# Delta-rule stage of a hybrid encoder layer: TensorE's order pinned over two streams, and the solved blocks turned on VectorE instead of through DRAM

## The chip, the cores and the metric

One core of a Trainium2 chip. The time is device microseconds of one execution of the whole kernel; the time of a kernel is the median of its runs. The profile comes from one further execution.

## The reference

One layer over 1024 positions of width 1024, in float32. The token mixing has a gated DeltaNet branch with 8 heads of 128 and a band attention branch with 16 heads; then come the branch projections, a LayerNorm, a gated feed-forward net with a short convolution, and another LayerNorm. The change lies in the DeltaNet branch:

```python
qkv = jax.nn.silu(causal_dwconv(qkv, conv_w))          # 4 taps
q = l2norm(q) * (A_DK ** -0.5); k = l2norm(k)
beta = sigmoid(beta_raw); g = -exp(a_log) * softplus(a_raw + dt_bias)
...
a_low = where(strict, einsum("bnhid,bnhjd->bnhij", k_beta, k) * decay, 0.0)
rhs = concatenate([v_beta, k_beta * exp(g)[..., None]], axis=-1)
sol = lax.linalg.triangular_solve(a_low + eye, rhs, left_side=True, lower=True, unit_diagonal=True)
u, w = sol[..., :dv], sol[..., dv:]
def step(state, inp):
    v_new = u_n - einsum("bhck,bhkv->bhcv", w_n, state)
    o_n = (einsum("bhck,bhkv->bhcv", q_n * exp(g_n)[..., None], state)
           + einsum("bhij,bhjv->bhiv", qk_n, v_new))
    state = state * exp(g_last)[..., None, None] + einsum("bhck,bhcv->bhkv", k_dec, v_new)
    return state, o_n
```

So each head has, chunk by chunk, the inverse of a unit lower triangular matrix and a recurrence over the chunks, which is serial. The kernel takes chunks of 128 positions, eight per head.

## The kernel before

Everything is held with channels on the 128 partitions. A projection multiplies in three passes: the input h and each weight block are split into a high and a low part (hh, hl; wh, wl), and `mm_fm` issues hh x wh, hl x wh and hh x wl for each of 8 pieces of the contraction. That makes 24 matmuls of 128x512 into one bank of PSUM, and 48 for a block of 128 output columns over 1024 positions. These matmuls (`pqkv`, `pz`, `pgt`, `pqk`, line L284) are the bulk of TensorE's work; they are called projection matmuls or dense matmuls here. The weight block comes by a DMA to `raw`; ScalarE casts it to `wh` (L177), and GpSimd subtracts to get `wl` (L180).

The delta-rule stage runs head by head. For a head:

- `stage_k`: decays `mm` and `gb` (L564 to L569, with an Exp of 128x1024 on ScalarE at L567), projection and convolution of k (`conv_in`, L554 is its Silu), transposes, the matrix `am` = k k^T with beta and decay; its 32x32 diagonal blocks go out to DRAM (`fa_d`, L609) and come back as `fa` (part of the buffer G) with one block per partition (L613). GpSimd puts -1 on their diagonals (L615).
- `stage_q`, `stage_vz`: the projections of q, v and z, transposes, scores `at`, scaled values `vs` (`pv`, L654).
- `stage_solve`: the 32 blocks (4 diagonal blocks in each of 8 chunks) are inverted row by row on VectorE: 31 times a TENSOR_TENSOR (L670) and a TENSOR_REDUCE (L672), each on the result of the one before. The result `ft` (FT) goes to DRAM in four writes (`ft_d`, L674) and comes back in four reads as blocks on the diagonal of `dt_` (part of G, L677), all on SP's DMA queue.
- `stage_inverse`, in two halves g of four chunks: VectorE transposes `dt_` to `dd` (L689), and four groups of small matmuls join 32x32 inverses to 64x64 and 128x128 ones: `pxt` (L694), `py` (L706 to L708), `pzz` (L714), `pT` (L720), with copies on ScalarE and VectorE between them (L697, L709 and their like).
- `stage_chain`: eight serial steps. In a step `pks` (L732) multiplies k by the state, VectorE updates `vs` (L733), `pvn` (L736) multiplies by the inverse, ScalarE copies to `vn` (part of SA, L739), `pu` (L742) makes the update, VectorE adds it to the state (part of SA, L747), and `po` (L750, L752) makes the output. Each of the three small matmuls pks, pvn and pu needs what an engine made of the one before; that is a hand-over, 168 in all.
- `stage_out`: the norm and the gate, and a DMA to `oa_d`.

The instructions are traced in this order: for a head h its solve, its inverse, some gate blocks (`some_gates`: projections of the merge gates and of two blocks for attention; GA says how many), k and q of head h+1, two half rows of the modulation (`mod_rows`), v and z of head h+1, the chain of head h and its output. A scheduler then sets the order on each engine by its own estimate of times, with the priorities PI, PC and PT for the inverse, the chain and the output. Nothing pins an engine's order but what `issue_after` ties. Buffers are rings of the size in the table `AT`: `xt`, `zd` and `dd` have two each.

Of the kernel before, what the change touches and what calls it, by code (L numbers as in the profile page):

```python
# [20 lines left out]
NK = 8  # L21
# [9 lines left out]
PI = 2000  # L31
PT = 2000
# [4 lines left out]
GE = ()  # L37
# [3 lines left out]
G0 = 1  # L41
GA = (3, 2, 2, 2, 3, 2, 2, 99)
# [12 lines left out]
GB = (0, 0, 0, 0, 0, 0, 0, 9)  # L55
# [7 lines left out]
def _at(group, step_, n, first=0):  # L63
# [15 lines left out]
    "tmp": tuple(_T), "dT": _at("G", 0, 1), "fa": _at("G", 0, 1, 1024), "dd": _at("G", 512, 2, 2048),  # L79
    "xt": _at("G", 256, 2, 3072), "zd": _at("G", 256, 2, 3584),  # L80
# [60 lines left out]
def hybrid_layer(  # L141
# [129 lines left out]
    def dhalf(name):  # L271
        return pbank(name, "d")
# [245 lines left out]
    def halves(name, col0, ready=None):  # L518

        w = None if ready else wblock(kview(w_in2, col0, P), NK)  # L520
        for n in range(2):
            ps = ready[n] if ready else dhalf(nm(name))
            if not ready:
                mm_fm(ps, w, hhk, hlk, n)
            yield n, slice(512 * n, 512 * n + 512), ps

    def conv_in(h, m):
        ti = m * NK + h
        y = big(f"y{m}")
# [19 lines left out]
        return y  # L549
# [6 lines left out]
    def stage_k(h):  # L556

        c = {}
# [12 lines left out]
        kT = c["kT"] = conv_in(h, 1)  # L571
        if h == 0:
            dump("kT", flat(kT))
        kd = c["kd"] = big("kd")
        ss = c["ss"] = sm("ss", 2 * NT)
        for g in range(2):
            pk = mbank("pk")
            for t in range(4):
                PE.transpose(pk[:, t, :], kT[:, 4 * g + t, :], ident)
            for t in range(4):  # L580
                u = 4 * g + t
                sumsq(ss[:, u:u + 1], pk[:, t, :])
            for t in range(4):
                u = 4 * g + t
                DVE.tensor_scalar(kd[:, u, :], pk[:, t, :], mm[:, u, P - 1:P], None, ALU.mult)
        kss = sm("kss")
        DVE.tensor_scalar(kss, ss[:, 0:NT], L2_EPS, None, ALU.add)
# [3 lines left out]
        bkk = sm("bkk")  # L591
# [4 lines left out]
        am = c["am"] = big("am")  # L596
        for g in range(2):
            pk = mbank("pkk")
            for t in range(4):
                PE.matmul(pk[:, t, :], kT[:, 4 * g + t, :], kT[:, 4 * g + t, :],  # L600
                          start=True, stop=True)
            for t in range(4):
                u = 4 * g + t
                DVE.scalar_tensor_tensor(am[:, u, :], pk[:, t, :], bkk[:, u:u + 1],
                                         mm[:, u, :], ALU.mult, ALU.mult)
        fa_d = scr.tile([4, NT, 32, 32], F32, tag="fa_d", bufs=2, name=nm("fa_d"))
        c["ft_d"] = scr.tile([4, NT, 32, 32], F32, tag="ft_d", bufs=2, name=nm("ft_d"))
# [10 lines left out]
        return c  # L618

    def stage_q(h, c):  # L620

        qT = c["qT"] = conv_in(h, 0)
        if h == 0:
            dump("qT", flat(qT))
        kT, mm, gb, ss = c["kT"], c["mm"], c["gb"], c["ss"]
        at = c["at"] = big("at")
        for g in range(2):
            G = slice(4 * g, 4 * g + 4)
            pk = mbank("pkq")
            for t in range(4):  # L630
                PE.matmul(pk[:, t, :], kT[:, 4 * g + t, :], qT[:, 4 * g + t, :],
                          start=True, stop=True)
            DVE.tensor_tensor(at[:, G, :], pk, mm[:, G, :], ALU.mult)
        for g in range(2):
            pk = mbank("pq")
            for t in range(4):
                PE.transpose(pk[:, t, :], qT[:, 4 * g + t, :], ident)
            for t in range(4):
                u = NT + 4 * g + t
                sumsq(ss[:, u:u + 1], pk[:, t, :], pk[:, t, :])  # L640
        eq = c["eq"] = sm("eq")
# [3 lines left out]
    def stage_vz(h, c):

        vT = conv_in(h, 2)
        if h == 0:
            dump("vT", flat(vT))
        vs = c["vs"] = big("vs")  # L650
        for g in range(2):
            pv = mbank("pv")
            for t in range(4):
                PE.transpose(pv[:, t, :], vT[:, 4 * g + t, :], ident)  # L654
            for t in range(4):
                u = 4 * g + t
                ACT.activation(vs[:, u, :], pv[:, t, :], AF.Copy, scale=c["bk"][:, u:u + 1])

        sz = c["sz"] = big("sz")
        for n, N, ps in halves("pz", 3 * D + h * P):  # L660
            ACT.activation(flat(sz)[:, N], ps, AF.Silu)

    def stage_solve(h, c):

        fa, ft_d = c["fa"], c["ft_d"]
        ft = ring("ft", [P, 8, 32])
        POOL.tensor_copy(ft, tt0)
        for i in range(1, 32):
            pr = ring("pr", [P, 8, 32])
            DVE.tensor_tensor(pr[:, :, 0:i + 1], ft[:, :, 0:i + 1],  # L670
                              fa[:, i:i + 1, 0:i + 1].to_broadcast([P, 8, i + 1]), ALU.mult)
            DVE.tensor_reduce(ft[:, :, i:i + 1], pr[:, :, 0:i + 1], AX.X, ALU.add, negate=True)  # L672
        for q in range(4):
            SP.dma_start(ft_d[:, :, 8 * q:8 * q + 8, :].rearrange("b t c j -> (b t) (c j)"),  # L674
                         ft[32 * q:32 * q + 32].rearrange("p c j -> p (c j)"))
        for b in range(4):
            SP.dma_start(dt_[32 * b:32 * b + 32, :, 32 * b:32 * b + 32],  # L677
                         ft_d[b].rearrange("t c j -> c t j"))

    def stage_inverse(h, c):  # L680
# [5 lines left out]
        for g in range(2):  # L686
            G = slice(4 * g, 4 * g + 4)
            dd = ring("dd", [P, 4, P])
            DVE.transpose(flat(dd), flat(dt_)[:, 512 * g:512 * g + 512])  # L689
            px_ = mbank("pxt", "i")  # L690
            for t in range(4):
                u = 4 * g + t
                for i, j in ((B0, B1), (B2, B3)):
                    PE.matmul(px_[i, t, j], am[:, u, i], dt_[:, u, j], start=True, stop=True)  # L694
            xt = ring("xt", [P, 4, 64])
            ACT.activation(xt[B0, :, 0:32], px_[B0, :, B1], AF.Copy, scale=-1.0)
            DVE.tensor_scalar(xt[B2, :, 32:64], px_[B2, :, B3], -1.0, None, ALU.mult)  # L697
            for b in (B2, B3):
                POOL.tensor_copy(am[b, G, b], dt_[b, G, b])
            POOL.memset(am[B1, G, B0], 0.0)  # L700
            POOL.memset(am[B3, G, B2], 0.0)
            for b in (B0, B1):
                POOL.tensor_copy(am[b, G, b], dt_[b, G, b])
            py = mbank("py", "i")
            for t in range(4):
                PE.matmul(py[B2, t, B3], dd[:, t, B2], xt[:, t, 32:64], start=True, stop=True)  # L706
                PE.matmul(py[B0, t, B1], dd[:, t, B0], xt[:, t, 0:32], start=True, stop=True)
                PE.matmul(py[B1, t, B0], xt[:, t, 0:32], dd[:, t, B0], start=True, stop=True)  # L708
            DVE.tensor_copy(am[B2, G, B3], py[B2, :, B3])  # L709
# [12 lines left out]

    def stage_chain(h, c):
# [3 lines left out]
        c["steps"] = []  # L727
        so = sm("so")
        for t in range(NT):
            if t:  # L730
                pks = mtile(nm("pks"), "c")
                PE.matmul(pks[:, 0:P], kT[:, t, :], st_, start=True, stop=True)  # L732
                DVE.scalar_tensor_tensor(vs[:, t, :], pks[:, 0:P], c["nbe"][:, t:t + 1],  # L733
                                         vs[:, t, :], ALU.mult, ALU.add)
            pv = mtile(nm("pvn"), "c")
            c["last"] = PE.matmul(pv[:, 0:P], am[:, t, :], vs[:, t, :], start=True, stop=True)  # L736
# [813 lines left out]
```

## Time and profile before

| | us |
|---|---|
| median of 3 runs | 2217.51 |
| lowest, highest | 2213.31, 2221.87 |
| the profiled execution | 2222.63 |
| its span in the trace | 2220.5 |
| TensorE busy in the span | 2140.7 (96%) |
| VectorE, ScalarE, GpSimd busy | 1477.9, 999.6, 500.9 |

The granted TensorE clock was 0.99 on average in the profiled execution. The page gives busy time by engine; times of single instructions are of that one execution. A busy time counts overlapped matmuls once: the 11577 matmuls take some 390 to 400 ns each by themselves (section 5), but start closer together. Idle time of an engine is put down to what came last before it could go on, written "<- engine tile line".

### The profile page before, as it was taken

The numbers are of one execution on the slowest core, as the hardware profiler recorded it, in microseconds if no ns is written. First come the engines' busy times: TensorE is split into PE (matmuls) and PEld (weight loads), VectorE is DVE, ScalarE is ACT, GpSimd is POOL, SyncE is SP. The second block draws the span as 40 slices with busy tenths as digits, with TensorE's granted clock in tenths as the row PEclk, the third lists the DMA queues.
The fourth block names the chain that finished last, engine by engine and source line by source line (L and its number), as shares of the span: only waits on it lengthen the run. The fifth ranks groups of instructions, "written<-read, shape, count | busy, mean of one in ns | idle before, by whom it ended". The sixth has DMA issues, their size and how long they took to land.

```text
span 2220.5 us, 31618 instructions
## 1 busy us (share of the span) xinstructions
PE 2140.7 (96%) x11577; PEld 1793.2 (81%) x11577; DVE 1477.9 (67%) x3096; ACT 999.6 (45%) x2127; POOL 500.9 (23%) x495
## 2 busy tenths in 40 slices
PE   7989999999999999999999899999999999999998
PEld 6778788777878787798989788888788888888886
DVE  6478476674758754567776653456998788875754
ACT  5634243443524334566765642234654444453331
POOL 0223233222323322233432422400120000000000
PEclk9999999999999999999999999999999999999999
DMA  9242323323243403211211424332232222275540
GB/s 289 86 121 71 113 80 106 110 74 110 78 120 87 128 24 99 68 51 50 72 55 60 148 96 128 114 128 95 76 102 70 78 83 86 90 260 210 171 152 38
DMA packets 227453, 232.01 MB, mean 104 GB/s; under 512 B 28058, under 2 KB 179027, under 8 KB 227299
## 3 DMA queue, kind: packets, MB, share of 16 engines
q1 hardware_dynamic: 227219, 229.98, 33.0%
q8 instruction: 91, 1.49, 0.3%
q14 instruction: 63, 0.52, 0.1%
q10 hardware_dynamic: 80, 0.03, 0.0%
HBM read 189.02 MB, written 47.23 MB: 106 GB/s over the span
## 4 chain that ended last, share of the span: by engine, by line
PE 49%; DVE 3%; ACT 1%; issue 1%; DMA 0%; POOL 0%; DVEq 0%; SPq 0%; ACTq 0%; POOLq 0%
PE pup L1268 17%; PE pdn L1422 11%; PE pbr L1049 8%; PE pwo L1110 4%; PE pqk L891 2%; PE pv L906 2%; PE po L981 2%; PE pp L966 1%; PE ps L940 1%; PE pn L1133 0%; DMA raw<-in_w_branch_a_dram 0%; DVE G L1329 0%; DVE t L170 0%; DVE kl L1011 0%; DVE pl L970 0%
## 5 line engine op out<-in xcount | busy, mean ns | idle before, releaser
L180 POOL TENSOR_TENSOR wl<-raw,wh 128x1024 fp32r<-128x1024 f32 x85 | 204.8, 2412 | 334.2 <-ACT wh L177 306.3
L1268 PE MATMUL pup<-hh,wop 128*128 128x512 f32 x704 | 224.2, 390 | 0.4 <-ACT G L1305 0.4
L1268 PE MATMUL pup<-t,wop 128*128 128x512 f32 x792 | 189.5, 392 | 1.4 <-DVE cc L1309 0.8
L1268 PEld LDWEIGHTS pup<-t,wop 128*128 128x128 f32 x792 | 148.6, 188 | 34.8 <-DVE cc L1309 1.2
L1422 PE MATMUL pdn<-dop,dop 128*128 128x512 f32 x696 | 161.6, 391 | 0.0
L177 ACT CAST wh<-raw 128x1024 fp32r<-128x1024 f32 x88 | 92.4, 1050 | 147.4 <-DMA raw<-in_w_in_dram 63.8
L1268 PEld LDWEIGHTS pup<-hh,wop 128*128 128x128 f32 x704 | 132.1, 188 | 29.1 <-ACT G L1305 0.8
L1422 PEld LDWEIGHTS pdn<-dop,dop 128*128 128x128 f32 x696 | 130.7, 188 | 28.3
L284 PE MATMUL pqkv<-hh,wh 128*128 128x512 f32 x352 | 142.8, 406 | 0.0
L284 PE MATMUL pqkv<-hl,wh 128*128 128x512 f32 x352 | 140.5, 399 | 0.0
L284 PE MATMUL pqkv<-hh,wl 128*128 128x512 f32 x352 | 140.2, 399 | 0.0
L1268 PE MATMUL pup<-hl,wop 128*128 128x512 f32 x352 | 137.2, 390 | 0.0
L670 DVE TENSOR_TENSOR FT<-FT,G 128x16 f32<-128x16 f32 (+30 forms) x248 | 121.6, 490 | 20.5 <-POOL G L615 13.1
L1310 POOL TENSOR_TENSOR cc<-cc,G 128x512 f32<-128x512 f32 x22 | 44.4, 2019 | 375.5 <-DVE G L1292 352.3
L951 POOL TENSOR_SCALAR G<-G,FT 128x640 f32<-128x640 f32 (+4 forms) x103 | 70.3, 685 | 182.4 <-DVE FT L950 161.6
L177 ACT CAST wop<-wr 128x512 fp32r<-128x512 f32 x104 | 61.9, 620 | 99.4 <-DVE wr L1250 66.9
L284 PE MATMUL pgt<-hh,wh 128*128 128x512 f32 x240 | 95.6, 399 | 0.4 <-DVE tmp L537 0.4
L284 PE MATMUL pgt<-hh,wl 128*128 128x512 f32 x240 | 94.7, 395 | 0.0
L284 PE MATMUL pgt<-hl,wh 128*128 128x512 f32 x240 | 94.7, 395 | 0.0
L180 DVE TENSOR_TENSOR wop<-wr,wop 128x512 fp32r<-128x512 f32 x104 | 75.3, 731 | 16.8 <-ACT wop L177 16.2
L970 DVE TENSOR_TENSOR pl<-pp,ph 128x512 fp32r<-128x512 f32 (+2 forms) x116 | 72.5, 635 | 17.4 <-ACT ph L969 16.6
L948 ACT ACTIVATE G<-G,FT 128x640 f32<-128x640 f32 (+4 forms) x103 | 71.6, 695 | 18.9 <-DVE FT L943 16.9
(413 smaller groups left out, 5786.2 us busy)
## 6 DMA issues: line engine op xcount, KB each, us to landing
raw<-in_w_in_dram SPq DMA_DIRECT2D x72, 512.0 KB
wr<-in_w_up_dram SPq DMA_DIRECT2D x44, 512.0 KB
dwr<-in_w_down_dram SPq DMA_DIRECT2D x44, 512.0 KB
raw<-in_w_ada_dram SPq DMA_DIRECT2D x32, 512.0 KB
wa<-in_w_ada_dram SPq DMA_DIRECT2D x32, 256.0 KB
gates_d<-GT SPq DMA_DIRECT2D x32, 256.0 KB
g_d<-G SPq DMA_DIRECT2D x15, 512.0 KB
rel_d<-in_rel_bias_dram SPq DMA_DIRECT2D x16, 383.5 KB
```

The lines of the kernel that those rows point to most:

```text
L177: he.copy(h, src)
L180: return le.tensor_tensor(l, src, f(h), ALU.subtract).ins
L284: i = PE.matmul(ps, a[:, k, :], r[k][:, 512 * n:512 * n + 512], start=(k == 0 and a is wh and r is rh), stop=(k == NK - 1 and a is wl))
L670: DVE.tensor_tensor(pr[:, :, 0:i + 1], ft[:, :, 0:i + 1], fa[:, i:i + 1, 0:i + 1].to_broadcast([P, 8, i + 1]), ALU.mult)
L891: PE.matmul(ps, a[:, k, :], r[:, k, 512 * n:512 * n + 512], start=(k == 0 and a is w[0] and r is hh), stop=(k == NK - 1 and a is w[1]))
L948: ACT.activation(sb[:, 0:n], sb[:, 0:n], AF.Exp, bias=mx[:, nb - 1:nb], scale=-1.0, accum_out=mx[:, 2:3])
L951: POOL.tensor_scalar(sb[:, 0:n], sb[:, 0:n], mx[:, 3:4], 0.0, ALU.mult, ALU.add)
L970: DVE.tensor_tensor(pl[:, B, :], pp, f(ph[:, B, :]), ALU.subtract)
L1049: PE.matmul(ps, a[:, k, :], r[k][:, N], start=(k == 0 and a is w[0] and r is rh), stop=(k == NK - 1 and a is w[1]))
L1110: PE.matmul(ps[n], a[:, t, k, :], wo[k][b][:, 512 * n:512 * n + 512], start=(k == 0 and a is mh and b == 0), stop=(k == NK - 1 and a is ml))
L1268: i = PE.matmul(ps, a[:, u, k, :], b[v][k], start=(new and k == 0 and u == 0 and v == 0), stop=(k == 3 and u == 1), skip_group_check=not new)
L1422: PE.matmul(ps[n], self.g[:, u, i * P:i * P + P], self.w[v][:, 512 * n:512 * n + 512], start=(first and u == 0 and v == 0), stop=(last and ...
```

## The change

- The solved blocks no longer go to DRAM. At the end of `stage_solve` VectorE transposes `ft` in 32x32 squares (L752 of the new file), eight copies on ScalarE (L758) and eight on VectorE (L760) put the rows in their places in `dd`, and four transposes on VectorE (L762) make `dt_`. `dd`, `dt_`, `xt` and `zd` have one buffer each and are cleared once at the start.
- The inverse takes all eight chunks of a head in one bank per step: four waves `pxt`, `py`, `pzz`, `pT` per head instead of eight groups. The number of matmuls is the same.
- Two streams are traced interleaved. `feed(h)` is a generator with the next head's projections (k, q, v, z, then gate blocks), its transposes, its modulation rows and, between gate blocks, its solve. `stage_inverse`, `stage_chain` and `stage_out` are generators that yield after each wave of small matmuls. For heads 0 to 6 a loop counts the projection matmuls (transposes count by their yields) and inserts the waves at given counts: the inverse at 38 and every 14 from there (`INV0`, `INVS`; 180 for head 0), the output of the head before at 14, 22 and 30, and the 23 waves of the chain from 56 behind the inverse's first wave on to 10 before the end (`WA`, `WB0`, `TAIL0`).
- `Lane` issues every matmul and transpose of this stage and, while `pinned` is set, keeps TensorE in the order of the trace (`tc.keep_in_program_order`). The output of head 6 and head 7's inverse, chain and output come behind that and are not pinned. The other engines' orders stay with the scheduler.
- The solve of a head is now traced with that head's own gates, which stand beside the chain of the head before. Three gate blocks are made with head 0 (G0), GA is changed to match, and the modulation rows are made a whole row at a time.

The core of the diff:

```diff
-G0 = 1
-GA = (3, 2, 2, 2, 3, 2, 2, 99)
+G0 = 3
+HM = 3
+GA = (3, 2, 2, 2, 2, 2, 1)
+INV0, INV00, INVS, OUT0, OUTS, TAIL0 = 38,180,14,14,8,10
+WA, WB0 = 9, 10
...
+    class Lane:
+        def __init__(self):
+            self.pinned = False
+        def __getattr__(self, op):
+            def call(*args, **kw):
+                r = getattr(PE, op)(*args, **kw)
+                return tc.keep_in_program_order(r) if self.pinned else r
+            return call
+    def project(ps, w, n):
+        for k in range(NK):
+            for a, r in ((w[0], hhk), (w[0], hlk), (w[1], hhk)):
+                lane.matmul(ps, a[:, k, :], r[k][:, 512 * n:512 * n + 512],
...
+                yield 1
...
     def stage_solve(h, c):
...
-        for q in range(4):
-            SP.dma_start(ft_d[:, :, 8 * q:8 * q + 8, :].rearrange("b t c j -> (b t) (c j)"),
-                         ft[32 * q:32 * q + 32].rearrange("p c j -> p (c j)"))
-        for b in range(4):
-            SP.dma_start(dt_[32 * b:32 * b + 32, :, 32 * b:32 * b + 32],
-                         ft_d[b].rearrange("t c j -> c t j"))
+        fr = ring("pr", [P, 8, 32])
+        DVE.transpose(fr.rearrange("p c j -> p (c j)"), ft.rearrange("p c j -> p (c j)"))
+        for b in (1, 3, 0, 2):
+            for q in range(4):
+                dst = dd[B[b], :, 32 * b + 8 * q:32 * b + 8 * q + 8]
+                s_ = fr[B[q], :, 8 * b:8 * b + 8].rearrange("p c t -> p t c")
+                if q % 2:
+                    ACT.copy(dst, s_)
+                else:
+                    DVE.tensor_copy(dst, s_)
+        for b in (1, 3, 0, 2):
+            DVE.transpose(dt_[B[b], :, B[b]], dd[B[b], :, B[b]])
 
     def stage_inverse(h, c):
...
-        for g in range(2):
-            G = slice(4 * g, 4 * g + 4)
-            dd = ring("dd", [P, 4, P])
-            DVE.transpose(flat(dd), flat(dt_)[:, 512 * g:512 * g + 512])
-            px_ = mbank("pxt", "i")
-            for t in range(4):
-                u = 4 * g + t
-                for i, j in ((B0, B1), (B2, B3)):
-                    PE.matmul(px_[i, t, j], am[:, u, i], dt_[:, u, j], start=True, stop=True)
...
+        px_ = ibank("pxt", 64)
+        for u in range(NT):
+            for i, j, o in ((B0, B1, slice(0, 32)), (B2, B3, slice(32, 64))):
+                lane.matmul(px_[i, u, o], am[:, u, i], dt_[:, u, j], start=True, stop=True)
...
+        yield
...
+    run(gate_block(0))
+    run(feed(0, G0, ()))
+    lane.pinned = True
+    older = None
+    for h in range(HA - 1):
+        fill, done = feed(h + 1, GA[h], (h, HA - 1)[:1 + (h == HM)]), 0
+        total = 4 * 48 + 48 * GA[h] + 32 + 4
+        if older is None:
+            waves = []
+        else:
+            waves = [(older, OUT0), (older, OUT0 + OUTS), (older, OUT0 + 2 * OUTS)]
+        inv, chain = stage_inverse(h, cs[h]), stage_chain(h, cs[h])
+        i0 = INV0 if h else INV00
+        waves += [(inv, i0 + INVS * i) for i in range(4)]
+        c0 = i0 + 4 * INVS
+        gaps = [WB0 if i % 3 == 0 else WA for i in range(22)]
+        pos = [sum(gaps[:i]) for i in range(23)]
+        waves += [(chain, c0 + (total - TAIL0 - c0) * p / pos[-1]) for p in pos]
+        for stream, at_ in waves:
+            while done < at_:
+                done += next(fill, total)
+            wave(stream, PC)
+        while wave(chain, PC):
+            pass
+        if older is not None:
+            while wave(older, PC):
+                pass
+        run(fill)
+        older = stage_out(h, cs[h])
+    lane.pinned = False
+    for stream in (older, stage_inverse(HA - 1, cs[-1]), stage_chain(HA - 1, cs[-1]), stage_out(HA - 1, cs[-1])):
+        while wave(stream, PC):
+            pass
```

How this moves instructions, at the end of the solve of head 3 and beside it. First VectorE before (the numbers behind names tell buffers and tiles apart; vs_2540 is head 2's):

```order
L670 TENSOR_TENSOR FT_670<-FT_670,G_93 128x256
L672 TENSOR_REDUCE FT_670<-FT_670 128x8
L733 SCALAR_TENSOR_TENSOR vs_2540<-pks_3502,SM_671,vs_2540 128x128
L823 TENSOR_SCALAR GT_673<-raw_4112,csil 128x512
L825 SCALAR_TENSOR_TENSOR GT_673<-raw_4112,csil,GT_673 128x512
L825 SCALAR_TENSOR_TENSOR GT_673<-raw_4116,csil,GT_673 128x512
L689 STREAM_TRANSPOSE G_93<-G_93 128x512 x2
```

The same place on VectorE now, where vs_2634 and pu_3678 belong to head 2's chain:

```order
L748 TENSOR_TENSOR FT_670<-FT_670,G_93 128x256
L750 TENSOR_REDUCE FT_670<-FT_670 128x8
L752 STREAM_TRANSPOSE FT_670<-FT_670 128x256
L760 COPY G_93<-FT_670 32x8x8 x8
L762 STREAM_TRANSPOSE G_93<-G_93 32x8x32 x4
L832 SCALAR_TENSOR_TENSOR SA_672<-SA_672,SM_671,pu_3678 128x128
L597 COPY SM_671<-tmp_3736 128x8
L817 SCALAR_TENSOR_TENSOR vs_2634<-pks_3698,SM_671,vs_2634 128x128
```

The turning (L752, L760, L762) stands right ahead of two of the chain's updates, where before modulation rows stood and the transposes behind the DMAs.

On TensorE before, a part of head 2's chain (vs_2540) beside head 3's inverse (am_3144):

```order
L284 MATMUL pqkv_4015<-hl,wh_4009 128x512
L284 MATMUL pqkv_4015<-hh,wl_4010 128x512
L736 MATMUL pvn_3519<-vs_2540,am_2312 128x128
L714 MATMUL pzz_3685<-am_3144 64x64 x4
L742 MATMUL pu_3522<-SA_672,kd_2280 128x128
L750 MATMUL po_3525<-SA_672,at_2415 128x128
L752 MATMUL po_3525<-SA_672,y_252_2344 128x128
L720 MATMUL pT_3692<-G_93 64x64 x4
L732 MATMUL pks_3530<-SA_672,y_238_2209 128x128
L694 MATMUL pxt_3699<-G_93,am_3144 32x32 x8
L736 MATMUL pvn_3533<-vs_2540,am_2312 128x128
L742 MATMUL pu_3536<-SA_672,kd_2280 128x128
```

On TensorE now, a part of head 2's chain (vs_2634, kd_2221) beside head 3's z projection (every matmul of the stage is issued by `Lane`, L525):

```order
L525 MATMUL pz_3358<-hh,wl_3353 128x512
L525 MATMUL pq_3398<-ident,y_321_2933 128x128 x4
L525 MATMUL pq_3407<-ident,y_321_2933 128x128 x4
L525 MATMUL pz_3418<-hh,wh_3352 128x512
L525 MATMUL pz_3418<-hl,wh_3352 128x512
L525 MATMUL pz_3418<-hh,wl_3353 128x512
L525 MATMUL pu_3422<-SA_672,kd_2221 128x128
L525 MATMUL po_3425<-SA_672,at_2514 128x128
L525 MATMUL po_3425<-SA_672,y_229_2109 128x128
```

Behind these come nine rows of pz, three of each of its kinds, and then head 2's next pks. Head 2's inverse had ended before its chain began, and head 3's begins behind this chain. Before, pvn, pu and pks of a chain stood there with only the small matmuls of the next head's inverse between them; now projection matmuls lie between any two of them.

More of the change, by code (lines that the diff above doesn't have):

```diff
@@ L645, in stage_vz, with scores @@
[L645 to L661, printed above, removed]
+    def scores(h, c, g):
+        G = slice(4 * g, 4 * g + 4)
+        pk = mbank("pkq")
+        for t in range(4):
+            lane.matmul(pk[:, t, :], c["kT"][:, 4 * g + t, :], c["qT"][:, 4 * g + t, :],
+                        start=True, stop=True)
+        DVE.tensor_tensor(c["at"][:, G, :], pk, c["mm"][:, G, :], ALU.mult)
@@ new lines, in stage_inverse @@
+        for b in (B2, B3):
+            POOL.tensor_copy(am[b, :, b], dt_[b, :, b])
+        POOL.memset(am[B1, :, B0], 0.0)
+        POOL.memset(am[B3, :, B2], 0.0)
+        for b in (B0, B1):
+            POOL.tensor_copy(am[b, :, b], dt_[b, :, b])
+        yield
+        py = ibank("py", 32)
+        for u in range(NT):
+            lane.matmul(py[B2, u, :], dd[:, u, B2], xt[:, u, 32:64], start=True, stop=True)
+            lane.matmul(py[B0, u, :], dd[:, u, B0], xt[:, u, 0:32], start=True, stop=True)
+            lane.matmul(py[B1, u, :], xt[:, u, 0:32], dd[:, u, B0], start=True, stop=True)
@@ new lines, in stage_inverse @@
+        DVE.tensor_copy(am[B2, :, B3], py[B2])
+        DVE.tensor_copy(dd[B1, :, B0], py[B1])
+        ACT.copy(am[B0, :, B1], py[B0])
+        yield
+        pz = ibank("pzz", 64)
+        for u in range(NT):
+            lane.matmul(pz[lo_, u], am[:, u, lo_], am[:, u, hi_], start=True, stop=True)
+        ACT.activation(zd[lo_], pz[lo_], AF.Copy, scale=-1.0)
+        POOL.memset(am[hi_, :, lo_], 0.0)
+        yield
+        pT = ibank("pT", 64)
+        for u in range(NT):
+            lane.matmul(pT[lo_, u], dd[:, u, lo_], zd[:, u], start=True, stop=True)
@@ L783, in qk_block, with use @@
     def qk_block(i):
[L785 removed]
+        def use(n, N, ps):
             gt_ = ring("gt", [P, 512])
@@ L873, in hybrid_layer @@
-    for t in GE:
-        with tc.issue_after(cs[-1]["steps"][t]):
-            some_gates(1)
+        yield
+        pr_ = mtile(nm("pmod"), "i")
+        lane.matmul(pr_, ones, acc, start=True, stop=True)
+        row = ring("gt", [P, 512])[0:1, :]
+        SP.dma_start(row, b_ada[:, C])
+        DVE.tensor_tensor(row, row, pr_[0:1, :], ALU.add)
+        SP.dma_start(mod_d[:, 512 * cb:512 * cb + 512], row)
+    cs = [{} for _ in range(HA)]
+    gates = iter([*range(1, 2 * NK), *((i,) for i in EP)])
@@ new lines, in run, with wave @@
+    def run(stream):
+        for _ in stream:
+            pass
+    def wave(stream, offset):
+        with tc.high_priority(offset=offset):
+            return next(stream, "end") != "end"
+    run(gate_block(0))
[27 more added lines that the diff above has]
+        older = stage_out(h, cs[h])
```

318 lines of the change are left out of this document (154 added, 164 removed).

## Prediction

> **What bounds the kernel now.** I read the page's busy shares first, then sums over stretches, then who waited for whom on TensorE, and last the order of time around the longest waits.
>
> ```profile
> PE 2140.7 (96%) x11577; PEld 1793.2 (81%) x11577; DVE 1477.9 (67%) x3096; ACT 999.6 (45%) x2127; POOL 500.9 (23%) x495
> ...
> 72.00:784.00 712.00, 681.86 (x4026) 561.75 (x4024) 483.41 (x1190) 291.27 (x795) 207.90 (x199) 0.99 0.34 98
> 784.00:930.00 146.00, 135.81 (x876) 117.53 (x875) 73.20 (x219) 59.76 (x165) 37.95 (x45) 0.96 0.18 56
> sum 858.00, PE 817.66 PEld 679.28 DVE 556.60 ACT 351.03 POOL 245.86; mean PE 408.83 PEld 339.64 DVE 278.30 ACT 175.51 POOL 122.93
> ```
>
> The columns of the stretches are length, then busy time of PE, PEld, DVE, ACT, POOL, then the granted clock. The delta-rule stage lies between 72 and 930 us; from 784 on the next stage's projections already fill in. TensorE is the bound throughout, so time is won only where it idles or runs at a lower clock. In this stage it idles 858.00 - 817.66 = 40.3 us: 30.1 us before 784 and 10.2 us after. Who ended those waits:
>
> ```profile
> PE pxt L694 <- DMA G<-ft_d: 14.4, 8, 6.7
> PE pks L732 <- DVE SA L747: 4.5, 3, 4.2
> PE pu L742 <- ACT SA L739: 3.3, 6, 1.1
> PE pvn L736 <- DVE vs L733: 3.2, 6, 0.9
> PE pv L654 <- ACT pq L554: 2.9, 2, 2.2
> ```
>
> (Total us, times, longest.) The largest is the first matmul of the block inverse, waiting for the solved blocks on their way through DRAM. In order of time:
>
> ```profile
> 158.79 0.39 PE L284 MATMUL pqkv<-hl,wh 128*128 128x512 f32 x1
> 159.02 0.39 PE L284 MATMUL pqkv<-hh,wl 128*128 128x512 f32 x1
> ...
> 166.54 0.99 PE L694 MATMUL pxt<-G,am 128*32 128x32 f32 x16 [6.68 <-DMA G<-ft_d]
> ...
> 424.02 0.25 PE L694 MATMUL pxt<-G,am 128*32 128x32 f32 x2 [2.12 <-DMA G<-ft_d]
> ...
> 425.70 0.75 PE L284 MATMUL pqkv<-hh,wh 128*128 128x512 f32 x1
> 426.25 0.63 PE L284 MATMUL pqkv<-hl,wh 128*128 128x512 f32 x1
> 426.68 0.63 PE L284 MATMUL pqkv<-hh,wl 128*128 128x512 f32 x1
> ...
> 788.39 0.79 PE L732 MATMUL pks<-SA,y 128*128 128x128 f32 x2 [4.15 <-DVE SA L747]
> ```
>
> A projection matmul costs 0.23 us from start to start (158.79 to 159.02), but 0.43 us after the wait at 424 (426.25 to 426.68). The granted clock tells the same:
>
> ```profile
> 159.00:170.00 11.00, 4.29 (x29) 3.26 (x28) 5.77 (x11) 6.62 (x15) 5.87 (x7) 0.69 0.66 169
> 421.00:430.00 9.00, 6.50 (x39) 4.99 (x39) 7.20 (x12) 1.77 (x6) 2.79 (x9) 0.81 0.68 184
> 784.00:795.00 11.00, 6.85 (x36) 6.64 (x35) 9.84 (x33) 3.16 (x11) 2.92 (x2) 0.69 0.00 0
> ```
>
> So a wait costs more than its length: 11 us at 0.69, 9 at 0.81 and 11 at 0.69 are 3.4, 1.7 and 3.4 us of clock lost, part of it while TensorE stood still anyway.
>
> **The change part by part.** The sum is made against the profiled execution: 2222.6 us, of it 2220.5 span. The median of the three runs, 2217.5, is 5.1 us lower, and I subtract the same gain from it.
>
> *Blocks turned on VectorE.* Eight transfers per head go (four out to ft_d, four back), and two transposes.
>
> ```profile
> 616.91 0.42 DVE L672 TENSOR_REDUCE FT<-FT 128x8 f32<-128x256 f32 x1
> 617.36 1.71 SPq L674 DMA_DIRECT2D ft_d<-FT  x4
> 620.30 1.80 SPq L677 DMA_DIRECT2D G<-ft_d  x4
> 623.55 1.30 DVE L689 STREAM_TRANSPOSE G<-G 128x512 f32<-128x512 f32 x2
> ...
> L689 DVE STREAM_TRANSPOSE G<-G 128x512 f32<-128x512 f32 x16 | 10.4, 691 | 18.8 <-DMA G<-ft_d 18.6
> L709 DVE COPY am<-py 32x128 f32<-32x128 f32 x16 | 4.6, 289 | 7.8 <-PE py L708 7.4
> L569 DVE COPY SM<-tmp 128x8 f32<-128x8 f32 x8 | 1.4, 172 | 5.1 <-ACT tmp L567 4.9
> ```
>
> The solve ends at 617.3 and the blocks are turned at 624.9. In their place come one transpose of 128x256 (half of L689: 0.35), eight copies of 32x64 on VectorE and eight on ScalarE (no such form here; between L569's 0.17 and L709's 0.29, say 0.2: 1.6 us on each) and four transposes of 32x256 (0.35 each, by the length of a row: 1.4). That is 3.4 us of VectorE per head, about 2.5 as a chain with ScalarE, against 1.4 removed. TensorE does not pay it: the first inverse wave stands 38 projection matmuls (38 x 0.23 = 8.7 us) into the next head's stream, behind the end of the solve, and the first head's stands 180 in. Without that cover (a solve 6 us late) the cost would be the lateness itself, at most the old 14.4 us. SP loses 64 issues; nothing else moves past them. So the 14.4 us go, and with them the clock lost behind them: between 0 and 3.4 + 1.7 = 5.1, of which the first falls half into idle time; I take 1.7 + 1.6 = 3.3.
>
> The Trainium skill, "TensorE: Matmul & The Clock Gate", section "What's actually happening", says that the clock falls to half after at least one idle window of about 3.4 us. By that rule the 2.12 us wait could not have done it, and the clock term would be 1.6 instead of 3.3; the trace has the half-speed matmuls right behind that wait, and I go by the trace.
>
> *Inverse in four waves per head.* Both halves of the head share one bank per step. The matmul count is the same; copies become half as many and twice as wide (L709 and its like), saving VectorE about 1 us per head off the path. TensorE: 0.
>
> *TensorE's order pinned, chain waves spread.* Before, of 168 hand-overs in the chain, 48 have no projection matmul between producer and consumer and the others mostly 10 to 20; now nearly all have 9 to 11, and none has 0. Small matmuls come in more groups (235 instead of 169), but a group alone or merged with another costs the same within noise, so I price that at 0. What the back-to-back hand-overs cost is in the 30.1 - 14.4 = 15.7 us of other waits before 784. These go, and new ones come. A hand-over now has 10 x 0.23 = 2.3 us, plus a small matmul. Against it stand four places in each head:
>
> ```profile
> 605.35 2.55 POOL L180 TENSOR_TENSOR wl<-raw,wh 128x1024 fp32r<-128x1024 f32 x1 [11.68 <-ACT wh L177]
> 610.70 2.40 POOL L180 TENSOR_TENSOR wl<-raw,wh 128x1024 fp32r<-128x1024 f32 x1 [2.80 <-ACT wh L177]
> ...
> 606.05 2.06 DVE L670 TENSOR_TENSOR FT<-FT,G 128x192 f32<-128x192 f32 x1
> 608.54 0.37 DVE L670 TENSOR_TENSOR FT<-FT,G 128x200 f32<-128x200 f32 x1
> 611.12 2.22 DVE L670 TENSOR_TENSOR FT<-FT,G 128x224 f32<-128x224 f32 x1
> ...
> L567 ACT ACT_TABLE_LOAD x8 | 10.3, 1283 | 0.1
> L567 ACT ACTIVATE tmp<-tmp 128x1024 f32<-128x1024 f32 x8 | 8.5, 1061 | 0.1
> L739 ACT COPY SA<-pvn 128x128 f32<-128x128 f32 x64 | 16.9, 263 | 49.5 <-PE pvn L736 49.0
> L747 DVE SCALAR_TENSOR_TENSOR SA<-SA,SM,pu 128x128 f32<-128x128 f32 x48 | 16.5, 343 | 22.1 <-PE pu L742 21.8
> ...
> 581.66 1.83 SPq L609 DMA_DIRECT2D fa_d<-am  x4
> 588.73 0.16 POOL L615 MEMSET G<- 128x32 f32 x1 [1.83 <-DMA G<-fa_d]
> ```
>
> (a) The next head's solve runs on VectorE during this head's chain, and the chain's updates (L832, L817 in the new file) are queued between its steps. A step that falls on a GpSimd pass takes 2.06 to 2.22 instead of 0.37, so all behind it is 1.8 us late; in 2.3 us the chain's own hand-over needs about 1.1. Bounds per pass: 0 (hidden) and 1.8. Some three passes fall into a solve; I take 1.0 per head. (b) The copy of vn (L739's successor) is queued on ScalarE behind one table load and three activations of 128x1024: 1.28 + 3 x 1.06 + 0.26 = 4.7 us. TensorE has eight projections (1.8 us) and eight transposes and pmod to do meanwhile. Bounds 0 and 2.9; since those others cover most of it, 0.5. (c) The last state update of the solve's stretch is queued behind the eight copies and four transposes: 3.0 against 2.3 plus a small group; bounds 0 and 0.7, I take 0.3. (d) The first step of the solve waits in VectorE's queue, ahead of a chain update, for the fa_d round trip, 7.1 us here (581.66 to 588.73); six hand-overs cover most of it: bounds 0 and 2, I take 0.3. Together 2.1 per head, 15 us for seven heads, against 15.7: a gain of 0.7. Bounds per head: 0.5 and 5.
>
> *Head 6 to head 7.* The wait of 4.15 us at 784 (the chain's update behind other VectorE work) is taken apart by the spread waves: with its clock between 0 and 7.5. The rest after 784 is scheduled as before. I take 3.
>
> Sum: 14.4 + 3.3 + 0.7 + 3 = 21.4 us. 2222.6 - 21.4 = 2201.2 for the profiled execution, 2217.5 - 21.4 = 2196.1 for the median. Outside 72 to 930 nothing is changed.
>
> **The rivals.** 0.5% of 2217.5, about what a measurement of this kernel can tell from no change, is 11.1 us.
>
> A, *new waits eat the gain*: at 5 us per head they cost 35 instead of 15.7, and 21.4 - 20 leaves 1.4: 2216. For it: the hand-overs are cut from mostly 10 to 20 matmuls to 9 to 11, while VectorE is 68% busy (483.41 of 712) in one queue. Against it: the places (a) to (d) reach 5 only when each comes near its upper bound.
>
> B, *GpSimd paces the chain* (slower): every pass over a solve goes through whole to TensorE, 3 x 1.8 = 5.4, and as the whole order behind is pinned nothing can step in; with 2 us for (b) to (d) 7.4 per head, 52 us for seven. That is 36 more than I allow: 2217.5 - 21.4 + 36.8 = 2233. It decides against the change from 6.8 us per head on (47.5 in all). For it: L670's 2.06 and 2.22. Against it: the updates between solve steps have 1 us of slack each. The Trainium skill, "Trainium Architecture — The Big Picture", section "What this means for kernel authors", calls the port that VectorE and GpSimd share an exclusive lock; taken to the letter it makes every pass count whole, which is this rival.
>
> C, *nearly all waits go*: 0.5 per head. 21.4 + 11.2 + the rest of the ends of the clock and of head 6 (1.8 + 4.5): 39, 2178. For it: no hand-over has less than its share of cover. Against it: (a) and (b) are long in every head.
>
> That the change does not do what it says is hardly open: the order on TensorE is fixed in the program. Only the turning could be slower than priced; it has 8.7 us of cover against 3.
>
> **How the numbers follow.** My forecast 0.52, A 0.22, B 0.10, C 0.16. Faster is forecast and C: 0.68; same is A: 0.22; slower is B: 0.10. The range leaves out the far half of B and a little of C: 2174 to 2224; the forecast's own is 2185 to 2206.
>
> **What would show it.** Right: no pxt wait over 0.5 us, no clock below 0.9 between 72 and 784, PE idle there about 15 us, the waits left on pu, pks and pvn at 0.3 to 1.5 us each. Wrong: several waits per head on the state update while a GpSimd pass runs (B), or waits on the vn copy of over 1 us in each head (A). What would make me wrong is slack misjudged: waits per head of 5 instead of 2.

## The result, and the profile after

The new kernel takes 2191.47 us in the median of four runs (2189.48 to 2194.31) against 2217.90 (2213.31 to 2221.87): 0.9883 of the time before, with an interval of 0.986 to 0.9905. Measured once more (run 9), beside nine runs of the kernel before, it took 2188.42 against 2220.38: 0.9859 (0.9845 to 0.9872). The profiled execution took 2189.48, with a span of 2187.8. It is the fastest of its four, and the profiled one of before was slower than the four runs beside it, so the spans differ by 32.7 us where the medians differ by 26.4 and 32.0. One execution of run 11 took 7455.93 us; that run's ratio is of its other four, its median is of all five.

The busy shares, then two stretches (columns as in the prediction) that meet at the end of the last z, as those of before did at 784, and hold together about the work of 72 to 930:

```profile
PE 2122.0 (97%) x11577; PEld 1778.3 (81%) x11577; DVE 1478.8 (68%) x3144; ACT 1013.7 (46%) x2173; POOL 492.8 (23%) x441
...
72.00:753.00 681.00, 663.82 (x3999) 547.44 (x3998) 487.69 (x1267) 305.07 (x842) 198.00 (x149) 0.99 0.33 99
753.00:897.00 144.00, 137.50 (x900) 119.54 (x899) 71.62 (x206) 62.36 (x167) 38.10 (x39) 0.99 0.23 70
```

4899 matmuls lie in these 825 us, 4902 in the 858 before. All the gain of 33 us is here: outside these stretches the two executions differ by 0.3 us. TensorE idles 23.7 us instead of 40.3, which is 16.7 of it. The other 16.3 us are busy time: 801.3 instead of 817.7 for nearly the same matmuls. Who ended the waits (total us, times, longest), from 72 to 930:

```profile
PE pvn L525 <- DVE FT L750: 3.7, 1, 3.7
PE pkk L525 <- DVE kd L610: 3.6, 1, 3.6
PE pks L525 <- DVE SA L832: 3.0, 6, 0.6
...
PE pvn L525 <- DVE vs L817: 1.8, 1, 1.8
...
PE pu L525 <- ACT SA L823: 0.7, 1, 0.7
```

No wait on the inverse's first matmul is left. In order of time, VectorE at the end of head 2's solve:

```profile
318.16 0.45 DVE L752 STREAM_TRANSPOSE FT<-FT 128x256 f32<-128x256 f32 x1
318.64 3.68 DVE L760 COPY G<-FT 32x64 f32<-32x64 f32 x8
322.35 1.84 DVE L762 STREAM_TRANSPOSE G<-G 32x256 f32<-32x256 f32 x4
324.22 0.35 DVE L832 SCALAR_TENSOR_TENSOR SA<-SA,SM,pu 128x128 f32<-128x128 f32 x1
```

GpSimd at the same time:

```profile
318.13 2.40 POOL L179 TENSOR_TENSOR wl<-raw,wh 128x1024 fp32r<-128x1024 f32 x1 [10.11 <-ACT wh L176]
```

And TensorE behind that, and at head 2's first inverse wave:

```profile
324.62 0.49 PE L525 MATMUL pks<-SA,y 128*128 128x128 f32 x2 [0.58 <-DVE SA L832]
...
340.45 0.70 PE L525 MATMUL pxt<-G,am 128*32 128x32 f32 x32
```

The turning takes 6.1 us (318.1 to 324.2), not the 2.5 to 3.4 that I priced. One of VectorE's eight copies took 1.96 us, beside the GpSimd pass of 2.40; the other seven took 0.20 to 0.32, about as priced. It does not matter: the blocks lie ready for 16.3 us before pxt asks for them. From the end of the solve to pxt there are 22.3 us, where I had counted a cover of 8.7, since the solve ends long before its head's stream does.

Where the busy time went shows in TensorE's own order. Before, in head 2's chain beside head 3's inverse:

```profile
433.70 0.39 PE L736 MATMUL pvn<-vs,am 128*128 128x128 f32 x2
434.33 0.65 PE L714 MATMUL pzz<-am 128*64 128x64 f32 x8 [0.24 <-ACT am L711]
434.91 0.49 PE L742 MATMUL pu<-SA,kd 128*128 128x128 f32 x2
435.24 0.39 PE L750 MATMUL po<-SA,at 128*128 128x128 f32 x2
435.46 0.39 PE L752 MATMUL po<-SA,y 128*128 128x128 f32 x2
435.77 0.68 PE L720 MATMUL pT<-G 128*64 128x64 f32 x8
436.38 0.49 PE L732 MATMUL pks<-SA,y 128*128 128x128 f32 x2
436.96 0.45 PE L694 MATMUL pxt<-G,am 128*32 128x32 f32 x16
437.41 0.46 PE L736 MATMUL pvn<-vs,am 128*128 128x128 f32 x2
438.22 0.49 PE L742 MATMUL pu<-SA,kd 128*128 128x128 f32 x2 [0.36 <-ACT SA L739]
```

And now, in a chain between projection matmuls:

```profile
318.35 0.38 PE L525 MATMUL pvn<-vs,am 128*128 128x128 f32 x2
318.49 0.48 PE L525 MATMUL pgt<-hh,wh 128*128 128x512 f32 x1
318.81 0.40 PE L525 MATMUL pgt<-hl,wh 128*128 128x512 f32 x1
319.04 0.40 PE L525 MATMUL pgt<-hh,wl 128*128 128x512 f32 x1
...
321.12 0.38 PE L525 MATMUL pu<-SA,kd 128*128 128x128 f32 x2
...
321.70 0.48 PE L525 MATMUL pgt<-hh,wl 128*128 128x512 f32 x1
```

A pvn between projections takes 0.14 us to the next start (318.35 to 318.49), and the projection behind it loses time too: it takes 0.32 to its follower (318.49 to 318.81) where 0.23 is usual (318.81 to 319.04). So the price of a pvn by itself is some 0.22 us. In the mixed run it takes 0.63 and 0.81 to the next start, of which 0.24 and 0.36 are idle. The whole run, 433.70 to 438.22, is 4.52 us with 0.60 idle. The same groups between projections, with what the projection behind them loses, each by its median over both kernels and runs 1 and 4 to 7 (0.22 for pvn and pks, 0.67 for pu and po, 0.57 for half a pxt, 0.80 and 0.81 for half a pzz and pT), come to 3.51. So 0.4 us of it is waiting that the page counts as busy. One place shows it: pks is counted as busy to 436.87, and pxt starts at 436.96, right behind VectorE's copy L721 (436.49 to 436.91), which it waits for.

Summed to the end of the last z, outside half-clock stretches and without idle time: before, 51 runs of mixed kinds took 93.7 us, where apart they would take 87.6; now 7 such runs take 13.6 against 14.0. That is 6 us. More comes from the number of groups. By the same medians the four whole groups of an inverse cost a head 4.19 us, eight half groups 5.50: 1.3 us per head, 9.2 for seven heads, and run 4 below, which has the half groups again, loses just that. These two make some 15 of the 16.3 us. The half clock behind the end of z, 3.4 us instead of 10.2, is a further part; as the stretches do not hold quite the same matmuls, the parts need not add up to the last microsecond.

### The profile page after: what moved, and what is told of

The parts are those of the page before. It is cut to its first block, busy times and chain, and to the rows that moved or that the text cites. A ratio compares the mean times of both kernels' runs of the same rounds, so it can differ in the third digit from the quotient of the medians.

```text
span 2187.8 us, 31581 instructions
## 1 busy us (share of the span) xinstructions
PE 2122.0 (97%) x11577; PEld 1778.3 (81%) x11577; DVE 1478.8 (68%) x3144; ACT 1013.7 (46%) x2173; POOL 492.8 (23%) x441
## 4 chain that ended last, share of the span: by engine, by line
PE 82%; DVE 10%; ACT 3%; DMA 2%; issue 1%; SPq 1%; POOL 0%; DVEq 0%; ACTq 0%; POOLq 0%
PE pup L1356 17%; PE pdn L1510 11%; PE pqkv L525 8%; PE pbr L1137 8%; PE pqk L979 6%; PE pv L994 4%; PE pwo L1198 4%; PE pgt L525 4%; PE pz L525 3%; PE po L1069 3%; PE ps L1028 2%; PE pp L1054 2%; DVE FT L748 2%; DVE FT L750 1%; PE pfirst L283 1%
## 5 line engine op out<-in xcount | busy, mean ns | idle before, releaser
L525 PE MATMUL pqkv<-hh,wh 128*128 128x512 f32 x352 | 143.2, 407 | 0.0
L525 PE MATMUL pqkv<-hl,wh 128*128 128x512 f32 x352 | 140.5, 399 | 0.0
L525 PE MATMUL pqkv<-hh,wl 128*128 128x512 f32 x352 | 140.5, 399 | 0.0
L748 DVE TENSOR_TENSOR FT<-FT,G 128x16 f32<-128x16 f32 (+30 forms) x248 | 103.9, 419 | 13.0 <-POOL G L647 5.9
L525 PE MATMUL pgt<-hh,wh 128*128 128x512 f32 x240 | 98.9, 412 | 0.0
L525 PE MATMUL pgt<-hh,wl 128*128 128x512 f32 x240 | 97.8, 407 | 0.0
L525 PE MATMUL pgt<-hl,wh 128*128 128x512 f32 x240 | 95.7, 399 | 0.0
L567 DVE SCALAR_TENSOR_TENSOR y<-pqkv,vt,y 128x511 f32<-128x511 f32 (+2 forms) x84 | 62.5, 744 | 44.3 <-ACT y L563 43.6
```

Of the source, the lines that this page charges most:

```text
L525: r = getattr(PE, op)(*args, **kw)
L748: DVE.tensor_tensor(pr[:, :, 0:i + 1], ft[:, :, 0:i + 1], fa[:, i:i + 1, 0:i + 1].to_broadcast([P, 8, i + 1]), ALU.mult)
```

## The experiments

Ratios stand against the kernel before, run on the same chip each time.

**1. The new kernel, blocks through DRAM again.**

```diff
-        fr = ring("pr", [P, 8, 32])
-        DVE.transpose(fr.rearrange("p c j -> p (c j)"), ft.rearrange("p c j -> p (c j)"))
...
+        for q in range(4):
+            SP.dma_start(ft_d[:, :, 8 * q:8 * q + 8, :].rearrange("b t c j -> (b t) (c j)"),
+                         ft[32 * q:32 * q + 32].rearrange("p c j -> p (c j)"))
...
+        for g in range(2):
+            DVE.transpose(flat(dd)[:, 512 * g:512 * g + 512], flat(dt_)[:, 512 * g:512 * g + 512])
```

> The new kernel, but the solved blocks go through DRAM again (four writes to ft_d, four reads, two transposes); TensorE's pinned order stays the same. Theory M (the order is what gains): in the new kernel's trace the blocks of heads 2 to 6 lie ready 14 to 16 us before the first pxt, and the path through DRAM took 7.6 us before against 6.1 to 6.5 us for the turning now, so the order covers the one as well as the other: 2191 to 2195 us, no pxt wait over 0.5 us but perhaps in head 7 (0.84 us of slack there). Rival D (the turning is what gains): the 14.4 us of waits on ft_d come back, 2205 us.

Measured: 2190.22 us, 0.9863 (0.9844 to 0.9881). Its VectorE at the end of head 2's solve:

```profile
319.24 0.42 DVE L750 TENSOR_REDUCE FT<-FT 128x8 f32<-128x256 f32 x1
326.81 1.30 DVE L759 STREAM_TRANSPOSE G<-G 128x512 f32<-128x512 f32 x2 [0.66 <-DMA G<-ft_d]
```

TensorE at head 2's first inverse wave, at 341.11 us, follows 13 us behind that. The waits, from 72 to 930:

```profile
PE pt L525 <- DVE at L846: 4.3, 3, 1.7
...
PE pks L525 <- DVE SA L829: 0.9, 2, 0.5
...
PE pxt L525 <- DMA G<-ft_d: 0.7, 1, 0.7
```

Through DRAM the blocks are ready at 328.1, 8.4 us after the solve, and still early. The 14.4 us of waits do not come back, and the time is that of the new kernel. Rival D falls: the turning gains nothing in this order. The waits on a state update are 0.9 us instead of 3.0, since 6 us of copies and transposes are gone from VectorE's queue; against that stand new waits of 4.3 us on `at`.

**2. The kernel before, turning alone.** `dd` is one buffer for the whole head.

```diff
-        for q in range(4):
-            SP.dma_start(ft_d[:, :, 8 * q:8 * q + 8, :].rearrange("b t c j -> (b t) (c j)"),
...
+        fr = ring("pr", [P, 8, 32])
+        DVE.transpose(fr.rearrange("p c j -> p (c j)"), ft.rearrange("p c j -> p (c j)"))
...
-            DVE.transpose(flat(dd), flat(dt_)[:, 512 * g:512 * g + 512])
+            dd = dd_[:, G, :]
```

> The kernel before with one change alone: the blocks are turned on VectorE and ScalarE, not through DRAM. TensorE's order stays the scheduler's (172 groups of small matmuls instead of 169, 174 changes of kind inside the groups instead of 179, 35 hand-overs without a projection matmul instead of 37). Theory M: the path from the solve's end to pxt gets 1 to 4 us shorter, so the 14.4 us of waits fall to between 2 and 12, all else stays: 2210 us (2205 to 2215). Rival D: the 14.4 us and their clock go altogether, 2200 us.

Measured: 2238.05 us, 1.0077 (1.0061 to 1.0093): slower. Both theories missed. The stretch to the end of the last z:

```profile
72.00:807.00 735.00, 696.08 (x4028) 569.63 (x4027) 507.21 (x1289) 310.26 (x850) 207.39 (x201) 0.97 0.31 93
```

The waits from 72 to 980:

```profile
PE pks L737 <- DVE SA L752: 5.9, 6, 2.1
PE pv L654 <- ACT pq L555: 5.8, 4, 2.4
PE py L711 <- DVE G L702: 5.7, 3, 4.8
PE pxt L699 <- DVE G L684: 5.4, 6, 3.5
```

The pxt wait falls from 14.4 to 5.4, but in an order without cover the copies on VectorE and ScalarE stand in front of other hand-overs, and TensorE idles 38.9 us instead of 30.1 up to the end of z. The clock then falls to 0.97, as ten half-clock stretches between 72 and 940 took the place of four. So in the scheduler's order, without that cover, the turning does not pay either. Which instruction each new wait stands behind I did not take apart.

**3. The new kernel, not pinned.**

```diff
-    lane.pinned = True
+    lane.pinned = False
```

> The new kernel with TensorE's order not pinned: the scheduler orders the same matmuls with the same priorities (157 groups, 162 changes of kind, 31 hand-overs without a projection matmul between). Theory M: the 14 us that TensorE won by fewer changes of kind are lost but for the some 5 us of the four waves, and hand-over waits of some 8 us come back: 2208 us (2200 to 2215). Rival D: turning and waves are still there, so 2192 to 2196 us.

Measured: 2293.03 us, 1.0327 (1.0309 to 1.0344), 100 us above the pinned one. Its waits from 72 to 980:

```profile
PE pk L525 <- ACT y L578: 24.1, 7, 4.9
PE pks L525 <- DVE SA L832: 19.6, 6, 3.9
```

Both theories expected far too little. The program text of the new kernel is written to be kept in order; given to the scheduler, TensorE stands still 66 us up to 850. Turning and waves are both still in it, and it is 71 us slower than the kernel before: they do not carry the gain without the order. How much of the loss is the missing pin and how much this text given to the scheduler, the run does not part.

**4. The new kernel, inverse in two halves.** Eight groups per head, pinned, 7 projection matmuls apart.

```diff
-        waves += [(inv, i0 + INVS * i) for i in range(4)]
+        waves += [(inv, i0 + INVS * i // 2) for i in range(8)]
```

> The new kernel with the inverse in two halves again, eight groups per head, each 7 projection matmuls apart, pinned. Theory M: by the groups in the two traces a half pxt costs TensorE 0.43 us, a half pzz or pT 0.70, against 0.72, 1.17 and 1.19 for whole ones; that is some 0.75 us per head and 5 us in all: 2196 us, the waits as in the new kernel. Rival W (the four waves are what TensorE's 14 us come from): 2205 us. If a group costs nothing, as the prediction had it: 2191 us.

Measured: 2216.06 us, 0.9977 (0.9965 to 0.9989): some 25 us above the new kernel. One head's stretch, in the new kernel and then with halves:

```profile
303.50:391.20 87.70, 87.11 (x542) 72.30 (x541) 64.47 (x168) 40.10 (x114) 26.62 (x20) 1.00 0.34 101
```

```profile
313.90:403.60 89.70, 88.62 (x541) 72.44 (x540) 64.88 (x171) 40.41 (x119) 26.97 (x27) 1.00 0.33 99
```

The same matmuls take 2.0 us more per head: 0.5 idle and 1.5 busy, 0.38 us for each of four groups more. By the end of z this is 16.1 us (769.5 against 753.4), of which 9.2 are busy time (673.0 against 663.8) and the rest idle, and 5 more come in head 7's part, which is not pinned. My 5 us had the groups too cheap, as they left out what the projection behind a group loses, and they left out the waits between halves that follow each other more closely. W's figure came nearest. Of its 14 us some 9 are the waves, in this order; the next run puts them into the old one.

**5. The kernel before, four waves alone.** Blocks through DRAM, the scheduler's order.

```diff
-        for g in range(2):
-            G = slice(4 * g, 4 * g + 4)
...
+        px_ = ibank("pxt", 64)
+        for u in range(NT):
```

> The kernel before with one change alone: the inverse of a head in four waves instead of eight groups; blocks through DRAM, the order the scheduler's (148 groups instead of 169, 185 changes of kind instead of 179, 38 hand-overs without a projection matmul between instead of 37). Theory W: in the pinned order an inverse group cost TensorE 0.37 us on top of its matmuls, so 32 fewer save 12 us whoever orders them: 10 to 12 us below the kernel before. Theory P (the pinned order is what lets the waves pay): waits on VectorE and ScalarE take their place, as they did when only the turning was changed: between 5 us below the kernel before and 20 above.

Measured: 2215.81 us, 0.9975 (0.9966 to 0.9984): 4.2 us less. Its waits, 72 to 930:

```profile
PE pxt L696 <- DMA G<-ft_d: 9.3, 7, 5.3
PE pvn L736 <- DVE vs L733: 7.2, 8, 1.4
PE pvn L736 <- DVE SM L543: 5.0, 6, 0.8
```

W falls, P holds. The mixed runs cost 8.6 us beyond the same groups apart (90.6 against 82.0), where before it was 6.1, and TensorE idles 31.3 us to the end of z instead of 30.1: waits on VectorE have taken the place of part of those on ft_d. So before to halves pinned is 0.9977, before to waves unpinned 0.9975, and both together 0.986. Each alone brings 4 to 6 us, together they bring 26 to 32. The places in run 4 were laid out for four waves; whether eight halves could stand better, and what pinning the old order alone is worth, no run shows.

**6 to 8. Places in the new order.** The second modulation row beside head 1; the inverse earlier, its waves sorted by place; and both.

```diff
-HM = 3
+HM = 0
...
-INV0, INV00, INVS, OUT0, OUTS, TAIL0 = 38,180,14,14,8,10
+INV0, INV00, INVS, OUT0, OUTS, TAIL0 = 10,180,14,14,8,10
...
+        waves.sort(key=lambda w_: w_[1])
```

> The new kernel with the second modulation row beside head 1 (HM = 0) and not head 4. Theory M: the waits of 3.7 and 1.8 us on pvn at 478 and 510 us come from VectorE's queue there, where that row's operations and two passes of 2.5 to 3.2 us beside GpSimd stand ahead of a chain's update. They go, and with them the 3.4 us of half clock behind them: 5 to 8 us less, 2184 us. Rival: such passes fall on another update instead, 2191 us.

> The new kernel with the inverse's first wave 10 instead of 38 projection matmuls into the next head's stream (heads 1 to 6; the waves sorted by their place), which spreads the chain's waves from 10 to some 11.3 matmuls. Theory M: of the 16.3 us that the blocks lie ready, 6.4 are used up, so no pxt wait comes, and the wait of 0.58 us on a state update in each head falls to 0.3 or less: 2188 us (2186 to 2191). Rival C (the prediction's: the 38 matmuls are the cover of the turning): 2.3 us of cover against 6.1 to 6.5 of turning are 4 us per head, 2215 us.

> The new kernel with both, HM = 0 and the inverse from 10 matmuls on. Theory M: the two gains add up, 2181 us (2178 to 2186). Rivals as told for each: 2191 or 2215 us.

Measured: 2188.93 us, 0.9858 (0.9841 to 0.9875); 2192.88, 0.9874 (0.9856 to 0.9891); 2194.11, 0.9877 (0.9858 to 0.9895). None can be told from the new kernel. With HM = 0 the two pvn waits at head 4 are gone, and beside head 1 this stands in their place:

```profile
PE pmod L525 <- ACT G L799: 4.4, 1, 4.4
...
PE pzz L525 <- ACT am L794: 2.9, 1, 2.9
```

So the time is the rival's, though the new waits stand on two copies on ScalarE and not on another update. With INV0 = 10 the blocks of heads 2, 3, 5 and 6 are still 9.3 us early and no pxt waits: my 38 matmuls were not the cover (rival C of that run falls). But the chain did not gain from wider gaps; its waits on a state update rose from 3.0 to 6.6 us. M was wrong in that.

**9 to 11. The last modulation row behind the pinned part**, with the new kernel beside it, and once more with the blocks through DRAM.

```diff
-        fill, done = feed(h + 1, GA[h], (h, HA - 1)[:1 + (h == HM)]), 0
+        fill, done = feed(h + 1, GA[h], (h,)), 0
...
     lane.pinned = False
+    run(mod_rows(HA - 1))
```

> The new kernel itself once more, on the same chip as the next two: 2189 to 2194 us by the first measurement.

> The new kernel with the last modulation row made behind the pinned part, beside head 7's chain, and not beside head 4 or head 1. Theory M: beside a pinned head the second row always costs 5 to 8 us of waits (5.5 at head 4, 7.3 at head 1); behind it the scheduler can put the row where nothing waits: the 5.5 us and up to 3.4 us of clock go, 2184 us (2181 to 2187). Rival: VectorE's queue beside head 7's chain is as full and the chain waits there instead, 2189 to 2193 us.

> The same, with the blocks through DRAM again. Theory M: as the order covers the path through DRAM as well, the same time as the version before it within 3 us; the waits of 0.58 us on a state update in each head go, since the copies and transposes behind the solve are gone from VectorE's queue. Rival D (the turning saves something that the waits don't show): 5 us or more above it.

Measured: 2188.42 us, 0.9859 (0.9845 to 0.9872); 2187.42, 0.9857 (0.9842 to 0.9872); 2190.04, 0.9855 (0.984 to 0.987). The second of them, to the end of z and on to 897:

```profile
72.00:743.00 671.00, 659.52 (x3996) 545.34 (x3995) 477.84 (x1258) 304.56 (x840) 194.97 (x148) 1.00 0.32 96
743.00:897.00 154.00, 138.92 (x876) 120.19 (x875) 72.09 (x200) 60.15 (x160) 39.77 (x39) 0.94 0.27 82
```

Its longest waits, from 72 to 930:

```profile
PE pv L995 <- ACT wh L176: 5.5, 1, 5.5
PE pv L995 <- DVE v L1002: 4.6, 1, 4.6
```

The 10 us up to the end of z are won as expected (671 us instead of 681) and given back wholly in the next 154: beside head 7's chain TensorE waits 5.5 and 4.6 us for attention's v, and the clock falls to 0.94. The rival holds, in another place than it named. Through DRAM the time is the same again. No version beats the new kernel by more than the runs scatter.

## Why the prediction was right, and where it was not

2191.47 lies 4.6 us from the forecast of 2196.1 and inside its range, and the forecast case is the one that came: the old waits go, and the new ones are few. That the figure came so near is in part luck. The sum was made against the profiled execution of before, and from there to the profiled one of now it is 33 us, not 21.4; in run 9 the medians too are 32.0 us apart. Term by term, against the profiled executions:

- *The ft_d waits, 14.4 us: right in size, wrong in cause.* They are gone, but run 1 keeps the DRAM path and does not have them. The order puts the end of the solve 22 us ahead of its inverse. "TensorE does not pay it" holds; the price of the turning was too low (6.1 us), and so was the cover (22.3 us, not 8.7).
- *The clock, 3.3 us: right in size, wrong in place.* In the stretch to the end of z, half-clock stretches of 6.8 and 3.4 us before stand against 3.4 and 6.8 now (from 171 and 482), where by my sign of being right there should be none. What was won lies behind it, where two (6.8 and 3.4) became one of 3.4.
- *"A group alone or merged with another costs the same within noise, so I price that at 0", and "TensorE: 0" for the four waves: this is the step that failed.* The merged groups cost 6 us of busy time, and the eight half groups instead of four whole ones 9.2. I had looked for such costs in the idle column alone. A hand-over that follows at once on TensorE hides part of its wait in busy time, and each group of its own takes time beside its matmuls.
- *New waits, 15 us against 15.7: right in sum, not in its parts.* Idle time to the end of z is 17.2 us. Beside the solves of heads 2, 3, 5 and 6 there is one wait of 0.5 to 0.6 us each, that of (c), near its upper bound of 0.7: in just these heads one of the copies took 1.96 to 1.99 us beside a GpSimd pass. (a), (b) and (d) cost nothing there. Instead the first head, whose feed is not pinned, has 6.7 us, and head 4, with two modulation rows, 5.5.
- *Head 6 to head 7, 3 us: about right.* Idle time behind the end of z fell from 10.2 to 6.5.
- *"Now nearly all have 9 to 11" was misread.* In the trace 89 of the 168 hand-overs have 9 to 11 projection matmuls. Those of head 0's chain have 5 to 7; one wait of 0.7 us, on pu, came there.

So the idle part of my 21.4 came out (16.7, against 14.4 + 0.7 and part of 3), and most of the busy part was missing. Rivals A and C did not come. B's mechanism did: in small in the four copies, and once in full, in head 4. VectorE there:

```profile
476.14 2.47 DVE L748 TENSOR_TENSOR FT<-FT,G 128x56 f32<-128x56 f32 x1
478.77 3.15 DVE L591 TENSOR_TENSOR tmp<-tmp,SB 128x1024 f32<-128x1024 f32 x1
```

GpSimd at the same time:

```profile
476.13 4.71 POOL L179 TENSOR_TENSOR wl<-raw,wh 128x1024 fp32r<-128x1024 f32 x2 [1.07 <-ACT wh L176]
```

And TensorE:

```profile
482.53 0.77 PE L525 MATMUL pvn<-vs,am 128*128 128x128 f32 x2 [3.71 <-DVE FT L750]
```

L591 takes 1.22 us in the seven other heads. Two slow operations had to stand one behind the other in a queue that also had the second modulation row, and run 6, which moves that row, has neither of the two pvn waits. In heads 2, 3, 5 and 6 the slow passes of the solve (two per head, of 1.1 and 2.1 us, where 0.3 is usual) were covered by the 9 to 11 matmuls of a hand-over.

## What to carry to other kernels

Before a transfer is replaced, look at whether an order that covers it is part of the same change: here the cover ended the waits, and the turning on the engines gained nothing or cost time. Idle time is not all that a serial hand-over costs: compare the start-to-start time of the same small matmuls alone and in a row, and count up to the second projection behind them, since the first is slower too. Parts of a change that gain 4 to 6 us each alone may gain some 30 together, so an undo of one part does not give its share.

## What was not expected of the hardware

*The clock falls after a window that is about half idle.* All half-clock stretches of a trace begin on one grid of 3.41 us and, but for the last, which the end of the trace cuts, last whole steps of it, one or two in most cases. The window before one of them, and that stretch, in the kernel before:

```profile
422.30:425.70 3.40, 1.30 (x22) 1.16 (x23) 3.07 (x5) 0.64 (x2) 1.48 (x6) 1.00 0.52 76
425.70:429.10 3.40, 3.40 (x11) 2.72 (x10) 3.27 (x7) 0.55 (x3) 0.91 (x3) 0.51 0.84 263
```

2.1 of 3.4 us idle were enough. Over the thirteen traces here, behind the first 13 us of each, windows at full clock with 1.95 us idle or more were followed by half clock without exception, those under 0.95 never, and between them both occur (1.93 us in run 4 was not, 0.99 in run 2 was). So a wait of 2.2 us can pass (one at 489 before, cut by the grid) or cost 1.7 us more. The Trainium skill, "TensorE: Matmul & The Clock Gate", section "What's actually happening", has the free-running window of 3413 ns, which the traces agree with, but asks for an idle window; here half a one did.

*A change to 32- or 64-wide tiles has a price of its own.* In the new kernel the start behind a projection matmul comes after 0.32 us for an inverse group and 0.23 for a chain group, and the next projection 0.13 to 0.15 behind the start of an inverse group's last matmul and 0.03 behind that of a chain's: 0.2 us per group. The 0.09 us that the projection behind either kind loses comes on top. The Trainium skill, "TensorEngine Tiling (Array Packing)", section "Key Properties", says that a change of tiling mode drains TensorE; the rows agree and give the size.

*Not every VectorE operation is slowed beside GpSimd.* L748 (both inputs in SBUF) took up to 2.6 us there, and the copies L760 up to 1.99 instead of 0.21; L817 and L832 (one input in PSUM) took at most 0.35 us in 37 such meetings, as elsewhere, and L750 at most 0.41, no more than elsewhere. The Trainium skill, "SBUF — State Buffer", section "Who interferes with whom", separates them in just this way. So the exclusive lock that rival B took to the letter never touched the chain's own updates, only what stood ahead of them in the queue.
